# First block's output projection computed in parts during the recurrence, partial sums kept in SBUF on top of x

## The chip, the core and the metric

The kernel runs on one core of one Trainium2 chip. The metric is the device time in microseconds of the whole program. The core has five engines that work side by side and hand work over by semaphores: TensorE (PE, matmuls), VectorE (DVE), ScalarE (ACT), GpSimd (POOL) and SyncE (SP), whose queue issues most DMAs. Each engine takes its instructions in the order in which the program was laid out for it.

## The reference

Two transformer blocks over 512 tokens of 1024 channels. Only the end of the first block's mixer and the start of its feed-forward part matter here:

```python
mod = silu(c) @ ada_w + ada_b
sh1, sc1, g1, sh2, sc2, g2 = split(mod, 6)
y, _ = rwkv_scans(r, k, v, w_lo, a_lo, lp, init)        # 8 heads, forward and backward recurrence, summed
y_conv = cb * shortconv1d(cc * cx)                       # 512 channels
y_rwkv = rwkv_output(y, r, k, v, g_lo, lp)               # group norm, bonus, gate: 512 channels
out_x = concatenate([y_conv, y_rwkv], -1) @ w_out        # 1024 -> 1024
x = x + g1 * out_x
hx = modulate(rms_norm(x, norm2_g), sh2, sc2)
x = x + g2 * conv_ffn(hx)                                # up 1024 -> 2 x 2816, 3x3 conv, silu gate, down
```

## The kernel before, in words

All activations lie transposed, as eight channel tiles of 128 partitions by 512 tokens. A large product is computed from float32 operands that are each split in a rounded "hi" and a remainder "lo": `split` makes hi on ScalarE (L181) and lo on VectorE (L182), and `mm3` issues three matmuls per 128 channels, hi by hi, lo by hi and hi by lo (L169 to L171). `wsplit` loads a weight into a tile of tag "w" on SP's queue (L156) and splits it into tiles "whi" and "wlo"; there are 3 buffers of "w" and 4 of each of the others.

`rwkv` runs the recurrence in four stages of two heads each, `stage(j)` for j from 0 to 3. A stage has 12 steps g, and in each a forward (d=0) and a backward (d=1) direction. One step of one direction is a chain: matmuls into `c1` (L762 with the state, L764 with the masked matrix `AS`), a copy `R` on ScalarE (L768), L770 with `XT` into `c1`, a copy `VU` (L771), L773 into `c2`, the new state `S` on ScalarE (L775), and the output matmuls L778. Every second step `pair` prepares two chunks for a direction: loads of `BKR` on SP's queue (L732), matmuls `psc` (L735), and the masked copy into `AS` on VectorE (L737), which a later step's L764 needs. The stage's group norm `gn(j)` runs beside the next stage's steps: `ys`, `gm`, `yc`, `ysq`, `gv`, a power `grs` on GpSimd, `yc` again, a transposition `py` (L835), the gate, and a split into `ahi[4+j]`, `alo[4+j]`. That of stage 3 has nothing to run beside.

Other work is pulled from a generator `todo`, `RB[j]` pieces per step, at a priority `PF[j]` behind the step's own; a scheduler lays out each engine's instructions by these priorities. In stages 2 and 3 `todo` holds `splits` (tiles 0 to 4 of the projection's input), `ada12` (32 loads of 512 KB of the modulation weight, each followed by one product with accumulation on VectorE, L544), and `first` (weights of two outputs). These share the "w", "whi" and "wlo" buffers; `ada12`'s vector `cb` keeps one "whi" buffer as long as `ada12` is not finished. The pool with these buffers is opened when stage 1 has been issued; its space becomes free during stage 2.

Behind the stages come three pieces of `gn(3)`, then k=0..6 of the outputs n=0 and 1, then the rest of the group norm. `out_proj1` loads x into `xin` on ScalarE's queue, finishes n=0 and 1 with k=7, and does n=2 to 7 with all k in two halves of 256 columns. Per output and half: eviction with gate and residual (L924), square and sum (L887, L888). Per half: a norm factor broadcast by `rsqrt_bc`, then `nt` (L929), `ahi` (L930), `alo` (L931) for the eight tiles. `ffn_up1` begins with four units in halves (`linear_halves`), so that their first halves run while the second half of `out_proj1` is normalized, and goes on with 512-column products.

Of the kernel before, what the change touches and what calls it, by code (L numbers as in the profile page):

```python
# [10 lines left out]
F32 = mybir.dt.float32  # L11
F32R = mybir.dt.float32r
I32 = mybir.dt.int32
AF = mybir.ActivationFunctionType
ALU = mybir.AluOpType
# [3 lines left out]
P = 128  # L19
NX = 512  # L20
NC_ = 256
NT = NX + NC_
KD = 8
# [99 lines left out]
class K:  # L123
# [5 lines left out]
    MU = [i / 18 for i in range(18)]  # L129
    MH = [(2.48 + i * 0.382) / 18 for i in range(45)]  # L130
    MT = [(11.955 + i * 0.234) / 18 for i in range(32)]
    PK, PG, PF = 200, 300, (110, 105, 118, 0)
    RB, RC = (4, 2, 1, 1), 5
    psa = None

    def __init__(self, tc, A):
# [341 lines left out]
    def rwkv(self, es, ep):  # L478
        nc, r2 = self.nc, self.r2
        st = lambda name, shape: r2.tile([P] + shape, F32, name=name)  # L480
        self.BKR = [[st(f"BKR{d}{i}", [2, 2, P]) for i in range(2)] for d in range(2)]
        self.AS = [[st(f"AS{d}{i}", [2, 2, P]) for i in range(2)] for d in range(2)]
        self.R = [[st(f"R{d}{i}", [P]) for i in range(2)] for d in range(2)]
        self.S0 = [st(f"S0{d}", [P]) for d in range(2)]
        self.C1 = [self.ps2.tile([P, 2, P], F32, name=f"c1{d}") for d in range(2)]
        self.C2 = [self.ps2.tile([P, P], F32, name=f"c2{d}") for d in range(2)]
        self.VU = [[st(f"VU{d}{i}", [P]) for i in range(3)] for d in range(2)]
        for t in (self.BKR[0][0], self.BKR[1][0], self.AS[0][0], self.AS[1][0], *self.R[0], *self.R[1], *self.VU[0], *self.VU[1], *self.S0):
            nc.vector.memset(t, 0.0)
        for t in (self.BKR[0][1], self.BKR[1][1], self.AS[0][1], self.AS[1][1], self.sets[2]["XT"]):  # L490
            nc.gpsimd.memset(t, 0.0)
        todo, gn = self.todo, iter(())
        for j in range(4):
            if j < 2:
                todo = chain(todo, self.prep(j + 2))
            gn = self.stage(j, self.S[j], todo, self.RB[j], gn)
            if j == 1:
                for _ in todo:
                    pass
                ep.close()  # L500
                self.wp = self.pool(es, "wp", side="right")
                self.mmbufs, self.axbufs, self.wbufs, self.wsbufs = 6, 2, 3, 4
                pa = self.pool(self.ea, "pmix", side="right")
                self.ahi = [pa.tile([P, NX], F32R, name=f"ahi{i}") for i in range(8)]
                self.alo = [pa.tile([P, NX], F32R, name=f"alo{i}") for i in range(8)]
                todo = chain(self.splits(), self.ada12(), self.first())
                self.e3 = es.enter_context(ExitStack())
                self.psa = self.psum(self.e3, "psa", side="right")
        for _ in todo:
            pass  # L510

        for _ in range(3):
            next(gn)
        for pm, w in self.ahead:
            self.mm3(pm, [(*w(k), self.ahi[k], self.alo[k]) for k in range(7)], last=False)
        for _ in gn:
            pass

    def splits(self):
        for k in range(5):  # L520
            self.split(self.ahi[k], self.alo[k], self.zx[k])
            yield

    def first(self):
        self.ahead = []
        for n in range(2):
            self.ahead.append((self.psax(), self.wsplit(self.A["wout"][n], KD, P)))
            yield

    def ada12(self):  # L530

        nc, wp = self.nc, self.wp
        tags = [("w", self.wbufs), ("whi", self.wsbufs), ("wlo", self.wsbufs)]
        cb, sb = (wp.tile([P, 1024], F32, tag=tags[i][0], name="cb", bufs=tags[i][1]) for i in (1, 2))
        nc.sync.dma_start(out=cb, in_=self.A["cb"])
        nc.scalar.activation(out=sb, in_=cb, func=AF.Tanh, scale=0.5)
        nc.vector.tensor_scalar(out=sb, in0=sb, scalar1=0.5, scalar2=0.5, op0=ALU.mult, op1=ALU.add)
        nc.vector.tensor_tensor(out=cb, in0=sb, in1=cb, op=ALU.mult)
        acc = wp.tile([P, 32], F32, name="adacc")
        for n in range(32):  # L540
            yield
            w, t = (wp.tile([P, 1024], F32, tag=tags[i][0], name="adaw", bufs=tags[i][1]) for i in (0, 2))
            nc.sync.dma_start(out=w, in_=self.A["adat"][n])
            nc.vector.scalar_tensor_tensor(out=t, in0=w, scalar=1.0, in1=cb, op0=ALU.mult, op1=ALU.mult, accum_out=acc[:, n:n + 1])  # L544
            if n in (7, 23, 31):
                a = 0 if n == 7 else 8 if n == 23 else 24
                nc.vector.tensor_tensor(out=self.mod[:, 16 + a:17 + n, 0], in0=acc[:, a:n + 1], in1=self.v("ada_b", 16 + a, n + 1 - a), op=ALU.add)

    def prep(self, j):
        nc, pp = self.nc, self.pp  # L550
# [294 lines left out]
    def tail(self):  # L845
        nc, A = self.nc, self.A
        with ExitStack() as es:
            self.bc = self.wp.tile([P, NX], F32, name="bc")
            self.bc1 = self.wp.tile([P, NX], F32, name="bc1")
            self.rt = self.wp.tile([P, 4], F32, name="rt")  # L850
            self.xr = self.zx
            self.ps = self.psum(self.e3, "ps3", side="right")
# [38 lines left out]
    def out_proj1(self):  # L891

        nc = self.nc
        g1, sh = self.mod[:, 16:24, 0], self.mod[:, 24:32, 0]
        G = self.q.tile([P, 16], F32, name="G2")[:, 0:KD]
        nc.vector.scalar_tensor_tensor(out=G, in0=self.mod[:, 32:40, 0], scalar=1.0, in1=self.v("norm2", 0, 8), op0=ALU.add, op1=ALU.mult)
        xin = [self.q.tile([P, NX], F32, name=f"xin{k}") for k in range(KD)]
        for k in range(KD):
            nc.scalar.dma_start(out=xin[k], in_=self.A["xT"][:, k, :])
        ws = []  # L900
        for n in range(2, KD):
            if n < self.WO:
                ws.append(self.wsplit(self.A["wout"][n], KD, P))
                continue
            w = self.wp.tile([P, KD, P], F32, tag="w", name="w", bufs=self.wbufs)
            nc.sync.dma_start(out=w, in_=self.A["wout"][n])
            hi, lo = (self.q.tile([P, KD, P], F32R, name=f"wo{t}{n}") for t in "hl")
            self.split(hi, lo, w)
            ws.append(lambda k, hi=hi, lo=lo: (hi[:, k, :], lo[:, k, :]))
        H = NX // 2  # L910
        for hf in range(2):
            c = slice(H * hf, H * hf + H)
            acc = None
            for n in range(KD):
                if n < 2:
                    if hf == 0:
                        pm, w = self.ahead[n]
                        self.mm3(pm, [(*w(7), self.ahi[7], self.alo[7])], first=False)
                        nc.vector.scalar_tensor_tensor(out=self.xr[n], in0=pm, scalar=g1[:, n:n + 1], in1=xin[n], op0=ALU.mult, op1=ALU.add)
                    acc = self.sumsq(acc, self.xr[n][:, c])  # L920
                    continue
                pm = self.psmm(H)
                self.mm3(pm, [(*ws[n - 2](k), self.ahi[k][:, c], self.alo[k][:, c]) for k in range(KD)])
                nc.vector.scalar_tensor_tensor(out=self.xr[n][:, c], in0=pm, scalar=g1[:, n:n + 1], in1=xin[n][:, c], op0=ALU.mult, op1=ALU.add)  # L924
                acc = self.sumsq(acc, self.xr[n][:, c])
            bc, _ = self.rsqrt_bc(acc, H, 1.0 / 1024, 1e-6, self.q)
            for k in range(KD):
                t = self.q.tile([P, H], F32, tag="nt", name="nt", bufs=2)
                nc.vector.scalar_tensor_tensor(out=t, in0=self.xr[k][:, c], scalar=G[:, k:k + 1], in1=bc, op0=ALU.mult, op1=ALU.mult)  # L929
                nc.scalar.activation(out=self.ahi[k][:, c], in_=t, func=AF.Identity, bias=sh[:, k:k + 1])  # L930
                nc.vector.scalar_tensor_tensor(out=self.alo[k][:, c], in0=t, scalar=sh[:, k:k + 1], in1=self.ahi[k][:, c].bitcast(F32), op0=ALU.add, op1=ALU.subtract)  # L931
# [36 lines left out]
    def ffn_up1(self):  # L968
        nc, u = self.nc, self.A["fup"]
        pms = self.linear_halves([u[0], u[FF], u[1], u[FF + 1]])  # L970
        for j in range(FF):
            pg = pms.pop(0) if pms else self.linear(u[j])
            acc = self.q.tile([P, NX], F32, tag="sq", name="cv", bufs=3)
            self.conv2d(j, pg, acc)
            nc.scalar.activation(out=acc, in_=acc, func=AF.Silu)
            pv = pms.pop(0) if pms else self.linear(u[FF + j])
            nc.vector.tensor_tensor(out=acc, in0=pv, in1=acc, op=ALU.mult)
            self.split(self.hid[j][0], self.hid[j][1], acc)

# [423 lines left out]
```

## Time and profile before

| | |
|---|---|
| time, median of 3 runs | 1631.62 us (1629.88 to 1634.76) |
| time of the profiled execution | 1632.26 us |
| span of the profiled execution | 1630.5 us |
| TensorE busy | 1551.8 us, 95% |
| VectorE busy | 1011.3 us, 62% |
| ScalarE busy | 702.0 us, 43% |
| granted TensorE clock, mean | 0.981 |

The span goes from the first to the last instruction; the time has 1.8 us around it. All times within the span are counted from its start. A busy TensorE is not TensorE at its peak: the recurrence's small matmuls count as busy while they wait for each other. Two parts of the span matter here: stage 3 of the recurrence, with the work that is pulled into it, and what lies between its last matmul and the FFN's steady run.

### The profile page before, as it was taken

To read this page: it belongs to the slowest core of one execution; us is meant where nothing else is said; L and a number is where in the kernel's file an instruction comes from. 1 tells how busy PE (TensorE), PEld (TensorE's weight loads), DVE (VectorE), ACT (ScalarE), POOL (GpSimd) and SP (SyncE) were. 2 spreads that over 40 slices of the span, in tenths; PEclk is the share of its full clock that TensorE was granted. 3 is DMA by queue.
4 is the path that set the end of the run, shared out by engine and by line. 5 is a ranking of instruction groups with operands and counts; after the bars stand their busy time and mean duration, and the time that the engine had idled before them with its cause. 6 is when DMAs were issued, how large, how long until landed. Compare 5 with 4: busy or idle time off the path is not lost. (4 is left out here: it accounts for less than half of the span.)

```text
span 1630.5 us, 23350 instructions
## 1 busy us (share of the span) xinstructions
PE 1551.8 (95%) x9054; PEld 1248.5 (77%) x9054; DVE 1011.3 (62%) x1710; ACT 702.0 (43%) x1402; POOL 159.6 (10%) x221
## 2 busy tenths in 40 slices
PE   4999999999999699999999998899999999999998
PEld 2777777777777599888888887787777888888886
DVE  3435767777765677888884437678975555555221
ACT  3424445776665443333333324335554333333122
POOL 1210002131213000000000003121210000000000
PEclk9999999999999899999999999999999999999999
DMA  9243423211136742323233332221012322233321
GB/s 328 85 150 98 141 80 96 59 42 24 38 115 193 234 156 78 101 93 103 92 97 86 95 98 81 78 65 52 27 53 90 98 97 91 91 96 97 103 80 63
DMA packets 85294, 160.77 MB, mean 99 GB/s; under 512 B 24512, under 2 KB 37568, under 8 KB 85184
## 3 DMA queue, kind: packets, MB, share of 16 engines
q1 hardware_dynamic: 81152, 152.34, 29.4%
q10 hardware_dynamic: 4032, 6.94, 1.3%
q8 instruction: 71, 1.16, 0.3%
q14 instruction: 39, 0.32, 0.1%
HBM read 143.00 MB, written 7.86 MB: 93 GB/s over the span
## 5 line engine op out<-in xcount | busy, mean ns | idle before, releaser
L181 ACT ACTIVATE whi<-w 128x1024 fp32r<-128x1024 f32 (+2 forms) x220 | 208.7, 950 | 458.5 <-PE pm L170 332.7
L182 DVE TENSOR_TENSOR wlo<-w,whi 128x1024 fp32r<-128x1024 f32 (+2 forms) x212 | 229.3, 1084 | 219.9 <-ACT whi L181 213.7
L169 PE MATMUL pm<-ahi,whi 128*128 128x512 f32 (+1 forms) x624 | 237.6, 381 | 3.2 <-DVE sh L1086 2.8
L170 PE MATMUL pm<-alo,whi 128*128 128x512 f32 (+1 forms) x624 | 235.9, 378 | 0.0
L171 PE MATMUL pm<-ahi,wlo 128*128 128x512 f32 (+1 forms) x624 | 235.0, 377 | 0.0
L170 PE MATMUL pm<-al,whi 128*128 128x512 f32 x352 | 139.7, 397 | 0.0
L169 PE MATMUL pm<-ah,whi 128*128 128x512 f32 x352 | 139.2, 395 | 0.0
L171 PE MATMUL pm<-ah,wlo 128*128 128x512 f32 x352 | 139.2, 395 | 0.0
L169 PEld LDWEIGHTS pm<-ahi,whi 128*128 128x128 f32 x624 | 118.3, 190 | 24.5 <-ACT sh L1101 3.2
L171 PEld LDWEIGHTS pm<-ahi,wlo 128*128 128x128 f32 x624 | 118.3, 190 | 20.9 <-issue 0.7
L170 PEld LDWEIGHTS pm<-alo,whi 128*128 128x128 f32 x624 | 118.4, 190 | 20.5 <-issue 0.6
L959 DVE SCALAR_TENSOR_TENSOR cv<-pm,vec,cv 128x441 f32<-128x441 f32 (+2 forms) x176 | 121.1, 693 | 4.1
L170 PEld LDWEIGHTS pm<-al,whi 128*128 128x128 f32 x352 | 66.2, 188 | 16.1 <-issue 0.2
L171 PEld LDWEIGHTS pm<-ah,wlo 128*128 128x128 f32 x352 | 66.2, 188 | 16.1 <-issue 0.2
L169 PEld LDWEIGHTS pm<-ah,whi 128*128 128x128 f32 x352 | 66.2, 188 | 15.9
L171 PE MATMUL pm<-hhi,wlo 128*128 128x512 f32 x176 | 72.5, 412 | 2.7 <-DVE wlo L182 2.7
L169 PE MATMUL pm<-hhi,whi 128*128 128x512 f32 x176 | 72.6, 413 | 0.2 <-ACT whi L181 0.2
L170 PE MATMUL pm<-hlo,whi 128*128 128x512 f32 x176 | 71.6, 407 | 0.0
L171 PE MATMUL pd<-whi,gl 128*128 128x512 f32 x176 | 69.3, 394 | 0.0
L169 PE MATMUL pm<-hh,whi 128*128 128x512 f32 x176 | 69.3, 394 | 0.0
L170 PE MATMUL pm<-hl,whi 128*128 128x512 f32 x176 | 69.3, 394 | 0.0
L171 PE MATMUL pm<-hh,wlo 128*128 128x512 f32 x176 | 69.3, 394 | 0.0
(403 smaller groups left out, 3082.8 us busy)
## 6 DMA issues: line engine op xcount, KB each, us to landing
w<-in_fup SPq DMA_DIRECT2D x44, 512.0 KB, 3.4
adaw<-in_adat SPq DMA_DIRECT2D x32, 512.0 KB, 4.4
w<-in_win SPq DMA_DIRECT2D x44, 256.0 KB, 2.8
w<-in_wg SPq DMA_DIRECT2D x22, 512.0 KB, 3.4
w<-in_wu SPq DMA_DIRECT2D x22, 512.0 KB, 3.4
w<-in_wd SPq DMA_DIRECT2D x22, 512.0 KB, 3.7
w<-in_win SPq DMA_DIRECT2D x18, 512.0 KB, 3.3
w<-in_wout SPq DMA_DIRECT2D x16, 512.0 KB, 3.5
```

The source lines that it names most:

```text
L169: nc.tensor.matmul(out, lh, rh, start=(first and i == 0), stop=False)
L170: nc.tensor.matmul(out, lh, rl, start=False, stop=False)
L171: nc.tensor.matmul(out, ll, rh, start=False, stop=(last and i == n - 1))
L181: self.nc.scalar.activation(out=hi, in_=src, func=AF.Copy)
L182: (eng or self.nc.vector).tensor_tensor(out=lo, in0=src, in1=hi.bitcast(F32), op=ALU.subtract)
L959: nc.vector.scalar_tensor_tensor(out=o, in0=p[:, ro[0] + dr:ro[1] + dr, co[0] + dc:co[1] + dc], scalar=w(i), in1=o, op0=ALU.mult, op1=ALU.add)
```

## The change

`fill` takes the place of `splits`, `ada12` and `first` as the filler of stages 2 and 3. It splits the tiles 0 to 4 and loads x again into the tiles that become free (`base`; three more tiles are new), with an `ada12` step each. Then it computes the output projection of all eight n in two passes, k=0..3 and k=4,5: a part of the weight is loaded and split, 12 or 6 matmuls of 512 columns go into a PSUM tile, and VectorE adds the tile, scaled by the gate g1, onto `base[n]`, followed by one `ada12` step. Last it loads and splits k=6 and 7 of all n in two tiles (`wlast`). `RB` and `PF` give two pieces a step in stages 2 and 3, and in stage 3 the same priority offset as in stage 2. `out_proj1` is left with k=6,7: six matmuls for each output and half, added to `base`. Its weight loads and the reload of x on ScalarE's queue go away. The last eight `ada12` steps move into `ffn_up1`.

```diff
-    PK, PG, PF = 200, 300, (110, 105, 118, 0)
-    RB, RC = (4, 2, 1, 1), 5
+    PK, PG, PF = 200, 300, (110, 105, 118, 118)
+    RB, RC = (4, 2, 2, 2), 5
...
-                todo = chain(self.splits(), self.ada12(), self.first())
+                self.mods = self.ada12()
+                todo = self.fill()
...
-        for _ in range(3):
-            next(gn)
-        for pm, w in self.ahead:
-            self.mm3(pm, [(*w(k), self.ahi[k], self.alo[k]) for k in range(7)], last=False)
...
+    def fill(self):
+        part = lambda n, k0, k1: self.wsplit(self.A["wout"][n][:, k0:k1], k1 - k0, P)
+        self.base = self.zx[0:5] + [self.wp.tile([P, NX], F32, tag=t, name="base", bufs=1) for t in ("bc", "bc1", "base")]
         for k in range(5):
             self.split(self.ahi[k], self.alo[k], self.zx[k])
+            nc.sync.dma_start(out=self.base[k], in_=self.A["xT"][:, k, :])
+            next(self.mods)
+            yield
+        for k in range(5, 8):
+            nc.sync.dma_start(out=self.base[k], in_=self.A["xT"][:, k, :])
+            next(self.mods)
+            yield
+        for k0, k1 in ((0, 4), (4, 6)):
+            for n in range(KD):
+                w = part(n, k0, k1)
+                pm = self.psax()
+                self.mm3(pm, [(*w(k - k0), self.ahi[k], self.alo[k]) for k in range(k0, k1)])
+                yield
+                nc.vector.scalar_tensor_tensor(out=self.base[n], in0=pm, scalar=self.mod[:, 16 + n:17 + n, 0], in1=self.base[n], op0=ALU.mult, op1=ALU.add)
+                next(self.mods)
+                yield
+        self.wlast = []
+        for i in range(2):
+            w = self.wp.tile([P, KD, P], F32, tag="w", name="w", bufs=self.wbufs)
+            nc.sync.dma_start(out=w.rearrange("p (n k) c -> p n k c", k=2), in_=self.A["wout"][4 * i:4 * i + 4, :, 6:8, :].rearrange("n p k c -> p n k c"))
...
-        for k in range(KD):
-            nc.scalar.dma_start(out=xin[k], in_=self.A["xT"][:, k, :])
...
                 pm = self.psmm(H)
-                self.mm3(pm, [(*ws[n - 2](k), self.ahi[k][:, c], self.alo[k][:, c]) for k in range(KD)])
-                nc.vector.scalar_tensor_tensor(out=self.xr[n][:, c], in0=pm, scalar=g1[:, n:n + 1], in1=xin[n][:, c], op0=ALU.mult, op1=ALU.add)
+                self.mm3(pm, [(*self.wlast[n](k), self.ahi[k][:, c], self.alo[k][:, c]) for k in (6, 7)])
+                nc.vector.scalar_tensor_tensor(out=self.xr[n][:, c], in0=pm, scalar=g1[:, n:n + 1], in1=self.base[n][:, c], op0=ALU.mult, op1=ALU.add)
...
             pv = pms.pop(0) if pms else self.linear(u[FF + j])
+            if j > 2:
+                next(self.mods, None)
```

The lines of the recurrence move down by 18 with the change: L770 becomes L788, L764 L782, L737 L755. On TensorE, in steps 2 and 3 of stage 3 before (c10 and c11 are the two directions' `c1`), the rows of the recurrence stand one behind the other:

```order
L770 MATMUL c10_2328<-R00_2322,XT0_83 64x64 x2
L764 MATMUL c11_2329<-VU12_2337,AS11_2321 64x64 x2
L766 MATMUL c21_2331<-S01_2327,cst_60 128x128
L773 MATMUL c20_2330<-VU02_2334,kbt_4807 128x128
L770 MATMUL c11_2329<-R10_2324,XT0_83 64x64 x2
L762 MATMUL c10_2328<-S00_2326,KR00_86 64x128
L773 MATMUL c21_2331<-VU12_2337,kbt_4818 128x128
L764 MATMUL c10_2328<-VU00_2332,AS01_2319 64x64 x2
```

At the same place of the changed kernel, on TensorE, px_4780 and px_4856 are the sums of the sixth and the seventh part:

```order
L171 MATMUL px_4780<-ahi3_4156,wlo_4777 128x512
L791 MATMUL c20_2330<-VU02_2334,kbt_5046 128x128
L782 MATMUL c11_2329<-VU12_2337,AS11_2321 64x64 x2
L169 MATMUL px_4856<-ahi0_4153,whi_4852 128x512
L170 MATMUL px_4856<-alo0_4161,whi_4852 128x512
L780 MATMUL c10_2328<-S00_2326,KR00_86 64x128
L788 MATMUL c11_2329<-R10_2324,XT0_83 64x64 x2
L782 MATMUL c10_2328<-VU00_2332,AS01_2319 64x64 x2
L171 MATMUL px_4856<-ahi0_4153,wlo_4853 128x512
```

Step 2's backward L788 now stands behind two matmuls of the seventh part. Its forward L788 stands in the fifth and the sixth part, step 3's forward one behind the ninth part, and step 6's behind five of the six matmuls of the fifteenth.

On VectorE, in stage 3 before, the masked copies for steps 6 and 7 (L737 into AS01 and AS11) stand between products of `ada12` (L544):

```order
L836 SCALAR_TENSOR_TENSOR zx_65<-py_4975,vec_61,zx_65 128x512
L544 SCALAR_TENSOR_TENSOR adaw_5077,adacc_4440<-adaw_5076,cb_4434 128x1024
L737 COPY_PREDICATED AS01_2319<-cst_60,psc_4985 128x512
L544 SCALAR_TENSOR_TENSOR adaw_5133,adacc_4440<-adaw_5132,cb_4434 128x1024
L737 COPY_PREDICATED AS11_2321<-cst_60,psc_4996 128x512
```

On VectorE of the changed kernel, at the same copies (L755), L182 is the split of a weight part, L535 the addition of a part's sum onto `base` or its reused tile, and L561 the product of `ada12`:

```order
L182 TENSOR_TENSOR wlo_5340<-w_5337,whi_5339 128x256
L535 SCALAR_TENSOR_TENSOR base_4227<-px_5268,mod_62,base_4227 128x512
L561 SCALAR_TENSOR_TENSOR adaw_5352,adacc_4239<-adaw_5351,cb_4233 128x1024
L182 TENSOR_TENSOR wlo_5388<-w_5385,whi_5387 128x256
L755 COPY_PREDICATED AS01_2319<-cst_60,psc_5280 128x512
L854 SCALAR_TENSOR_TENSOR zx_65<-py_5256,vec_61,zx_65 128x512
L561 SCALAR_TENSOR_TENSOR adaw_5400,adacc_4239<-adaw_5399,cb_4233 128x1024
L755 COPY_PREDICATED AS11_2321<-cst_60,psc_5291 128x512
```

The copy for step 6 stands behind the split of the sixteenth and last part (wlo_5388). The split of the first part stands behind stage 2's group norm up to its second `yc`.

## Rows read from the trace of the kernel before

**Rows 1.** Page, part 1: busy time, share of the span, instructions.

```profile
PE 1551.8 (95%) x9054; PEld 1248.5 (77%) x9054; DVE 1011.3 (62%) x1710; ACT 702.0 (43%) x1402; POOL 159.6 (10%) x221
```

**Rows 2.** Windows view, all engines; clock, DMA share, GB/s last.

```profile
core 0: us, PE busy (x) PEld busy (x) DVE busy (x) ACT busy (x) POOL busy (x), PEclk, DMA share, GB/s
491.00:551.60 60.60, 59.11 (x456) 44.13 (x454) 35.77 (x62) 35.64 (x121) 16.25 (x22) 1.00 0.64 199
551.60:564.00 12.40, 0.07 (x1) 0.10 (x2) 9.87 (x21) 1.96 (x3) 1.64 (x1) 0.66 0.76 236
564.00:569.60 5.60, 5.60 (x17) 4.43 (x18) 3.99 (x6) 1.69 (x2) 0.00 (x0) 0.54 0.88 278
626.40:640.00 13.60, 13.60 (x112) 13.43 (x111) 8.48 (x13) 5.54 (x6) 0.00 (x0) 1.00 0.27 86
640.00:860.00 220.00, 220.00 (x972) 182.09 (x971) 188.66 (x252) 81.32 (x104) 0.00 (x0) 1.00 0.30 97
```

**Rows 3.** Timeline of TensorE; start, duration, what ran, idle before it.

```profile
492.18 0.45 PE L770 MATMUL c<-R,XT 128*64 128x64 f32 x4
...
504.48 0.45 PE L770 MATMUL c<-R,XT 128*64 128x64 f32 x4
...
521.66 0.45 PE L770 MATMUL c<-R,XT 128*64 128x64 f32 x4
...
551.12 0.45 PE L778 MATMUL c<-VU,AS 128*64 128x64 f32 x4 [0.36 <-ACT VU L771]
...
563.93 0.66 PE L835 MATMUL py<-cst,yc 128*128 128x128 f32 x2 [12.36 <-DVE yc L831]
```

**Rows 4.** Windows view, VectorE's instructions of line L544 alone.

```profile
491.00:551.60 60.60, 25.33 (x41) 1.00 0.64 199
551.60:564.00 12.40, 6.42 (x12) 0.66 0.76 236
```

**Rows 5.** Waits of SP's queue, 460 to 630: total, times, longest.

```profile
SPq L543 <- DVE adaw L544: 40.1, 19, 4.7
```

**Rows 6.** Timeline of VectorE.

```profile
494.63 0.69 DVE L818 TENSOR_REDUCE gm<-ys 128x8 f32<-128x512 f32 x1 [1.52 <-POOL ys L815]
...
505.43 0.69 DVE L831 TENSOR_TENSOR yc<-yc,grs 128x512 f32<-128x512 f32 x1 [2.50 <-POOL grs L830]
...
569.09 0.69 DVE L182 TENSOR_TENSOR alo<-zx,ahi 128x512 fp32r<-128x512 f32 x1 [0.62 <-ACT ahi L181]
...
595.22 0.48 DVE L924 SCALAR_TENSOR_TENSOR zx<-pm,mod,xin 128x256 f32<-128x256 f32 x1 [1.43 <-PE pm L171]
...
599.55 0.87 DVE L929 SCALAR_TENSOR_TENSOR nt<-zx,G,nbc 128x256 f32<-128x256 f32 x2 [0.79 <-PE nbc L208]
```

**Rows 7.** Page, part 6: DMA issues, KB each, median us to landing.

```profile
adaw<-in_adat SPq DMA_DIRECT2D x32, 512.0 KB, 4.4
...
w<-in_win SPq DMA_DIRECT2D x44, 256.0 KB, 2.8
```

**Rows 8.** VectorE by line and form, 467 to 660: busy, mean ns.

```profile
L544 DVE SCALAR_TENSOR_TENSOR adaw<-adaw,cb 128x1024 f32<-128x1024 f32 x32 | 39.7, 1253 | 4.0 <-DMA adaw<-in_adat 4.0
...
L182 DVE TENSOR_TENSOR wlo<-w,whi 128x1024 fp32r<-128x1024 f32 x15 | 18.3, 1223 | 11.2 <-ACT whi L181 10.9
...
L931 DVE SCALAR_TENSOR_TENSOR alo<-nt,mod,ahi 128x256 fp32r<-128x256 f32 x16 | 7.1, 482 | 0.9 <-ACT ahi L930 0.9
...
L929 DVE SCALAR_TENSOR_TENSOR nt<-zx,G,nbc 128x256 f32<-128x256 f32 x16 | 7.0, 476 | 1.6 <-PE nbc L208 1.6
...
L888 DVE TENSOR_TENSOR acc<-acc,sq 128x256 f32<-128x256 f32 x14 | 5.8, 421 | 2.7 <-ACT sq L887 2.7
...
L924 DVE SCALAR_TENSOR_TENSOR zx<-pm,mod,xin 128x256 f32<-128x256 f32 x12 | 5.8, 481 | 4.0 <-PE pm L171 3.8
```

**Rows 9.** DMA issues of 467 to 563, KB each, median us to landing.

```profile
BKR<-KR SPq DMA_DIRECT2D x16, 64.0 KB, 3.3
...
BKR<-KR SPq DMA_DIRECT2D x4, 32.0 KB, 5.6
```

More of the change, by code (lines that the diff above doesn't have):

```diff
@@ L510, in rwkv @@
             pass
-        for _ in range(3):
-            next(gn)
-        for pm, w in self.ahead:
-            self.mm3(pm, [(*w(k), self.ahi[k], self.alo[k]) for k in range(7)], last=False)
         for _ in gn:
             pass
-    def splits(self):
+    def fill(self):
+        nc = self.nc
+        part = lambda n, k0, k1: self.wsplit(self.A["wout"][n][:, k0:k1], k1 - k0, P)
+        self.base = self.zx[0:5] + [self.wp.tile([P, NX], F32, tag=t, name="base", bufs=1) for t in ("bc", "bc1", "base")]
         for k in range(5):
             self.split(self.ahi[k], self.alo[k], self.zx[k])
+            nc.sync.dma_start(out=self.base[k], in_=self.A["xT"][:, k, :])
+            next(self.mods)
             yield
[L524 to L527, printed above, removed]
+        for k in range(5, 8):
[15 more added lines that the diff above has]
+            nc.sync.dma_start(out=w.rearrange("p (n k) c -> p n k c", k=2), in_=self.A["wout"][4 * i:4 * i + 4, :, 6:8, :].rearrange("n p k c -> p n k c"))
+            hi, lo = (self.wp.tile([P, KD, P], F32R, tag=f"w{t}", name=f"w{t}", bufs=self.wsbufs) for t in ("hi", "lo"))
+            self.split(hi, lo, w)
+            self.wlast += [lambda k, hi=hi, lo=lo, n=n: (hi[:, 2 * n + k - 6, :], lo[:, 2 * n + k - 6, :]) for n in range(4)]
             yield
@@ L540, in ada12 @@
         for n in range(32):
-            yield
             w, t = (wp.tile([P, 1024], F32, tag=tags[i][0], name="adaw", bufs=tags[i][1]) for i in (0, 2))
@@ L847, in tail @@
         with ExitStack() as es:
-            self.bc = self.wp.tile([P, NX], F32, name="bc")
-            self.bc1 = self.wp.tile([P, NX], F32, name="bc1")
+            self.bc = self.wp.tile([P, NX], F32, tag="bc", name="bc", bufs=1)
+            self.bc1 = self.wp.tile([P, NX], F32, tag="bc1", name="bc1", bufs=1)
             self.rt = self.wp.tile([P, 4], F32, name="rt")
@@ L896, in out_proj1 @@
         nc.vector.scalar_tensor_tensor(out=G, in0=self.mod[:, 32:40, 0], scalar=1.0, in1=self.v("norm2", 0, 8), op0=ALU.add, op1=ALU.mult)
-        xin = [self.q.tile([P, NX], F32, name=f"xin{k}") for k in range(KD)]
-        for k in range(KD):
-            nc.scalar.dma_start(out=xin[k], in_=self.A["xT"][:, k, :])
[L900 to L909, printed above, removed]
         H = NX // 2
@@ L914, in out_proj1 @@
             for n in range(KD):
[L915 to L921, printed above, removed]
                 pm = self.psmm(H)
-                self.mm3(pm, [(*ws[n - 2](k), self.ahi[k][:, c], self.alo[k][:, c]) for k in range(KD)])
-                nc.vector.scalar_tensor_tensor(out=self.xr[n][:, c], in0=pm, scalar=g1[:, n:n + 1], in1=xin[n][:, c], op0=ALU.mult, op1=ALU.add)
+                self.mm3(pm, [(*self.wlast[n](k), self.ahi[k][:, c], self.alo[k][:, c]) for k in (6, 7)])
+                nc.vector.scalar_tensor_tensor(out=self.xr[n][:, c], in0=pm, scalar=g1[:, n:n + 1], in1=self.base[n][:, c], op0=ALU.mult, op1=ALU.add)
                 acc = self.sumsq(acc, self.xr[n][:, c])
```

## The prediction

> **What bounds the kernel now.** The page gives TensorE 95% of the span [rows 1], so I looked for the stretch where it is not doing useful work and cut the program there with the windows view [rows 2]. From 640 to 860 us (the FFN's up projection) TensorE is full: 972 matmuls in 220.00 us, 0.226 us for a 512-column matmul at full clock, with VectorE at 188.66. Between the last recurrence matmul (551.12, ended at 551.6) and the first matmul behind it (563.93, after 12.36 us idle) [rows 3] nothing can run, as only the group norm of stage 3 is left; VectorE is busy 9.87 of those 12.40 us [rows 2], and 6.42 of that are `ada12` products (L544) [rows 4]. Then comes `out_proj1` up to 640.
>
> In stage 3 itself, 491 to 551.6, TensorE's busy figure is 59.11 of 60.60 [rows 2], but it holds only 456 instructions: the recurrence is a chain TensorE, ScalarE, TensorE. Step 0 has its L770 at 492.18, step 3 at 504.48, step 6 at 521.66, the end is at 551.6 [rows 3]: 4.1 us a step at first, and 29.9 from step 6 to the end. The filler is not free either: SP stood 40.1 us in 19 waits for a tile that VectorE had not yet read (L543 behind L544) [rows 5], with three "w" buffers.
>
> **The change, part by part.** Its sign is a difference of two numbers: how much later the recurrence ends, and how much less is left behind it.
>
> *What it puts into stage 3.* Sixteen parts: 8 outputs with k=0..3 (12 matmuls each) and 8 with k=4,5 (6 each), 144 × 0.226 = 32.6 us of TensorE. Each brings a load, a split on ScalarE and VectorE, an addition on VectorE and an `ada12` step. Although `fill` is available from stage 2 on, the pool opens late there, so nearly all of it falls into stage 3. TensorE's order shows the serious part: step 2's L788 stands inside the 5th to 7th part, step 3's behind the 9th, step 6's first behind the 15th. VectorE's shows pair 3's masked copy, which step 6 needs, behind the 16th split. An engine that takes its rows in order then ties the recurrence to the fill.
>
> When does the 16th split come? *Start.* The first split stands behind stage 2's group norm, whose `gm` starts at 494.63 and whose last `yc` ends at 506.1 now [rows 6]. Two products and a copy fewer lie in that chain then (3 us), one product and the split behind it (2 us): about 504. *Pace.* Three buffers carry two loads per part. A product's buffer is held for 4.4 us of landing [rows 7] and 1.25 of VectorE [rows 8], 5.65; a 256 KB part for 2.8 [rows 7] and two conversions of about 0.69 (the 569.09 row [rows 6]; ScalarE's taken like it), 4.2. With about 1 us of hand-overs that is 10.85 over 3 buffers, 3.6 us per part. Before, these buffers allowed a product each (4.4 + 1.25) / 3 = 1.9 us, and 41 records, two to a product, in 60.6 us [rows 4] make 2.95, as SP also waits for the recurrence's own loads; so I take 4.0 for the first eight. The halves of the second pass land in 2.8 (256 KB [rows 7]) to 3.3 us (64 KB [rows 9]) and split in 0.42 (as L888's 128x256 row [rows 8]): 5.65 + 3.05 + 0.84 + 1 over 3, 3.5, taken as 3.6. The 16th split then is at 504 + 8 × 4.0 + 7 × 3.6 = 561. Bounds: below, VectorE's own work, 1.25 + 0.69 + 0.69 and 1.25 + 0.42 + 0.69 per part, together 40 us, so 544; above, every landing as slow as the 5.6 us of the 32 KB loads in this stretch [rows 9], (5.6 + 1.25 + 5.6 + 1.4 + 1) / 3 = 4.95 × 15, so 578.
>
> From there: masked copy and step 6's first matmuls to its L788 1.6, then five steps and 2.4 for the rest of the last. A step is 4.1 where little lies beside it and (29.9 - 2.4) / 5 = 5.5 from step 6 on now [rows 3]; I take the middle, 4.8, as products and the last parts still lie there: 26.4. The recurrence ends at 589 instead of 551.6, **37.4 us later** (4.1: 33.9, 5.5: 40.9).
>
> Here a rule stands against the change. Step 3's L770 rows ran at 504.48 as soon as their data came [rows 3], with no held matmul ahead of them. The Trainium skill ("TensorE: Matmul & The Clock Gate", section "Architectural detail: the array is 16× 32×32, not 1× 128×128") says that TensorE's queue can pull weight loads ahead of matmuls in flight but is otherwise no free reordering, and that VectorE is strictly first in, first out. By it the recurrence waits for the parts as above, and the sum stands. Without holding, the parts would cost the recurrence at most ScalarE's sixteen splits ahead of its copies, 8 × 0.69 + 8 × 0.42 = 9 us: 9 - 29.4 = -20.4, about 1611.
>
> *What it takes from behind.* (1) Group norm: no products in its chain, 12.36 less 6.42 [rows 3, 4], **6.4 us**. (2) From the last `alo` (569.09 + 0.69 = 569.8 [rows 6]) to 640 are 70.2 us. Now 6 instead of 24 matmuls remain per output and half, and VectorE sets the pace: 16 evictions of 0.481, 14 sums of 0.421, 16 each of `nt` and `alo` at 0.48 (0.476 and 0.482) make 28.9 [rows 8], two weight splits of the FFN at 1.223 make 2.4, start 1.0. The chain between the halves shows 595.22 + 0.48 to 599.55 [rows 6], 3.85, in which two sums (0.84) and two small rows (about 0.5) ran: 2.5 idle, twice. Sum 37.3 to the last normalized tile. Behind it now lie 13.6 us [rows 2]; then the second halves of three units, 3 × 24 matmuls of 256 columns at 0.12, are 8.6, and 1.3 for a weight buffer that `cb` still holds. So 47.2 instead of 70.2, **23.0 us**; at 13.6 behind it, 19.3. (3) The reload of x moves from ScalarE's queue to SP's, where the loads of `fill` wait anyway: in the pace.
>
> *What it moves further.* Eight products go to `ffn_up1`: 8 × 1.25 = 10 us on VectorE, which has 220.00 - 188.66 = 31 us free there [rows 2]. I take nothing; if no gap could be used it would be 10.
>
> **Sum.** +37.4 - 6.4 - 23.0 = +8.0. The profiled execution took 1632.26, so 1640.3; on the median of three, 1631.62, it is 1639.6. A difference of 0.3% (4.9 us) is about what a measurement of this kernel can tell from none. Break-even is a recurrence that ends 29.4 us late, that is a 16th split at 553.
>
> **Rivals.**
> - *The fill runs at VectorE's pace.* If landings overlap better than three buffers suggest, the 16th split comes at 544, the recurrence ends at 572, 20.4 late: 9 us gained, about 1623. For it: the DMA share of 0.64 in stage 3 leaves room [rows 2]. Against: SP's 40.1 us of waits for buffers [rows 5]. If ready recurrence matmuls were also not held, the time would be the 1611 worked out above. The rival holds from a 16th split before 548: 0.24.
> - *Balance.* Split between 548 and 558, end of the sum within 4.9 us of zero, 1627 to 1636: 0.20.
> - *Much slower.* TensorE falls to half clock. Where it waited for VectorE (551.6 to 564) the granted clock was 0.66, and 0.54 after it to 569.6 [rows 2], the lower level of 1.2 GHz; a 512-column matmul then takes about 0.45. In stage 3 twelve of them would take 5.4 us, more than the 4.0 of pace: eight times 1.4 is 11 us, 1650. In the tail, where TensorE now waits for VectorE, the 72 last matmuls would cost 8.6 more, 1648. Slow landings (578) give 1656. Against the clock falling: in stage 3 it was 1.00 throughout [rows 2]. The Trainium skill, same page, section "HAM oscillation — how this bites in real kernels", describes bursts of matmuls between waits for loads that pay for the cold array each time; 12 matmuls (2.7 us) and a pause of 1.3 look like it, but the recurrence lies between them. 0.14.
>
> **How the numbers follow.** The forecast (16th split between 558 and 570) has 0.42, and its own range is 1636.5 to 1648. Faster 0.24, same 0.20, slower 0.42 + 0.14 = 0.56. The range of 8 in 10 goes from 1619 (a little beyond VectorE's pace) to 1652.
>
> **What would show it.** Step 3's L788 near 537 to 542 instead of 504.5; SP's waits for "w" buffers as the largest; pair 3's copy directly behind the 16th split at about 561; last L796 at about 589; then 6 us less to the first `py`, and about 47 us from the last `alo` to where the FFN's 512-column matmuls run without gaps; in the FFN no new wait of TensorE for VectorE. I am wrong if parts follow each other at 3 us or less, if recurrence matmuls run far ahead of the parts that stand before them, or if the tail takes more than 52 us.

## The result and the profile after

The changed kernel takes 1641.79 us (median of 4 runs, 1641.57 to 1643.09) against 1631.14 us: a ratio of 1.0062, 95% interval 1.0047 to 1.0077. It is slower by 10.7 us; 8.0 were forecast. The span of the profiled execution is 1639.9 us, 9.4 more than before.

The timeline of TensorE shows the recurrence of stage 3 and what follows it; the rows answer to [rows 3], and L788, L796, L853 are the old L770, L778, L835.

```profile
493.56 0.45 PE L788 MATMUL c<-R,XT 128*64 128x64 f32 x4
497.62 0.45 PE L788 MATMUL c<-R,XT 128*64 128x64 f32 x4
...
519.57 0.33 PE L788 MATMUL c<-R,XT 128*64 128x64 f32 x2
...
522.92 0.33 PE L788 MATMUL c<-R,XT 128*64 128x64 f32 x2
...
534.76 0.45 PE L788 MATMUL c<-R,XT 128*64 128x64 f32 x4
...
560.08 0.45 PE L788 MATMUL c<-R,XT 128*64 128x64 f32 x4
...
590.73 0.45 PE L796 MATMUL c<-VU,AS 128*64 128x64 f32 x4 [0.36 <-ACT VU L789]
598.03 1.08 PE L853 MATMUL py<-cst,yc 128*128 128x128 f32 x4 [6.86 <-DVE yc L849]
...
647.99 0.40 PE L169 MATMUL pm<-ahi,whi 128*128 128x512 f32 x1
```

These are steps 0, 1, 2 (in two halves), 3 and 6, the end of the recurrence, the first matmul behind it, and the first 512-column matmul of the FFN, which stood at 639.00 before. The recurrence ends at 591.2 instead of 551.6. TensorE then idles 6.86 us instead of 12.36.

The timeline of VectorE has the first, ninth and sixteenth split of a weight part, the masked copy that step 6 needs, and the last tile of the input and of the output of `out_proj1`:

```profile
504.62 0.69 DVE L182 TENSOR_TENSOR wlo<-w,whi 128x512 fp32r<-128x512 f32 x1
...
532.16 0.42 DVE L182 TENSOR_TENSOR wlo<-w,whi 128x256 fp32r<-128x256 f32 x1
...
556.71 0.42 DVE L182 TENSOR_TENSOR wlo<-w,whi 128x256 fp32r<-128x256 f32 x1
557.04 0.73 DVE L755 COPY_PREDICATED AS<-cst,psc 128x512 f32<-128x512 int32 x1
...
601.33 0.69 DVE L182 TENSOR_TENSOR alo<-zx,ahi 128x512 fp32r<-128x512 f32 x1 [0.70 <-ACT ahi L181]
...
637.48 0.94 DVE L929 SCALAR_TENSOR_TENSOR alo<-nt,mod,ahi 128x256 fp32r<-128x256 f32 x2 [0.19 <-ACT ahi L928]
```

The windows view, with the columns of [rows 2], shows stage 3, the group norm's stretch, `out_proj1` and the FFN:

```profile
500.00:520.00 20.00, 16.47 (x79) 12.48 (x80) 13.63 (x26) 4.95 (x11) 1.94 (x2) 1.00 0.69 215
520.00:540.00 20.00, 20.00 (x105) 15.42 (x106) 14.31 (x25) 6.78 (x19) 1.81 (x3) 1.00 0.74 229
540.00:560.00 20.00, 19.96 (x137) 15.57 (x135) 14.38 (x26) 9.62 (x31) 1.99 (x5) 1.00 0.59 186
560.00:580.00 20.00, 19.73 (x158) 14.77 (x156) 9.24 (x12) 13.80 (x41) 3.10 (x7) 1.00 0.48 156
591.20:598.20 7.00, 0.17 (x1) 0.20 (x2) 3.79 (x7) 0.90 (x2) 1.64 (x1) 0.59 0.00 0
...
602.00:638.40 36.40, 32.80 (x218) 31.07 (x218) 28.02 (x70) 15.70 (x34) 1.39 (x2) 0.85 0.09 30
660.00:860.00 200.00, 200.00 (x884) 165.58 (x883) 177.42 (x243) 74.09 (x94) 0.00 (x0) 1.00 0.38 121
```

In stage 3 TensorE is busy throughout from 520 on, with fewer instructions per 20 us while the parts run. Before, it also filled `out_proj1`, as the windows view of that kernel shows from the input's last tile on:

```profile
569.80:626.40 56.60, 55.66 (x423) 53.41 (x422) 37.90 (x75) 23.34 (x42) 1.39 (x2) 1.00 0.38 126
```

Now it no longer does (32.80 of 36.40). VectorE is busy almost throughout from 605 to 625, and the clock falls again behind that:

```profile
605.00:625.00 20.00, 16.39 (x113) 14.83 (x113) 18.28 (x47) 11.18 (x24) 0.69 (x1) 0.93 0.01 1
625.00:630.00 5.00, 5.00 (x25) 5.00 (x25) 1.69 (x4) 0.00 (x0) 0.69 (x1) 0.50 0.66 210
```

The FFN stays full although VectorE has more to do there.

By stretches, in us: the recurrence ends 39.6 later; from there to the last `alo` of the input (602.0) it is 10.8 instead of 18.2; from there to the FFN's first 512-column matmul 46.0 instead of 69.2; from that to the end of the span 991.9 instead of 991.5. Sum: +39.6 - 7.4 - 23.2 + 0.4 = +9.4.

### The profile page after: what moved, and what is told of

The parts are those of the page before. It is cut to its first block, busy times and chain, and to the rows that moved or that the text cites. A ratio compares the mean times of both kernels' runs of the same rounds, so it can differ in the third digit from the quotient of the medians.

```text
span 1639.9 us, 23242 instructions
## 1 busy us (share of the span) xinstructions
PE 1557.0 (95%) x8958; PEld 1247.7 (76%) x8958; DVE 1021.9 (62%) x1738; ACT 704.3 (43%) x1412; POOL 155.0 (9%) x221
## 5 line engine op out<-in xcount | busy, mean ns | idle before, releaser
L181 ACT ACTIVATE whi<-w 128x1024 fp32r<-128x1024 f32 (+3 forms) x234 | 215.1, 920 | 471.5 <-PE pm L170 337.2
L182 DVE TENSOR_TENSOR wlo<-w,whi 128x1024 fp32r<-128x1024 f32 (+3 forms) x226 | 235.8, 1045 | 219.2 <-ACT whi L181 213.7
L169 PE MATMUL pd<-whi,gh 128*128 128x512 f32 x176 | 69.5, 395 | 0.0
```

Of the source, the lines that this page charges most:

```text
L169: nc.tensor.matmul(out, lh, rh, start=(first and i == 0), stop=False)
L181: self.nc.scalar.activation(out=hi, in_=src, func=AF.Copy)
L182: (eng or self.nc.vector).tensor_tensor(out=lo, in0=src, in1=hi.bitcast(F32), op=ALU.subtract)
```

## The experiments

"Stage 3" is here the time from step 0's first L770 (L788) to the end of the last output matmul, read from the timeline of TensorE; it does not contain shifts from earlier stages. It is 59.4 us before and 97.6 after, each from one profiled execution. In the run with twelve float32 matmuls behind it, where the stage itself is as before, it is 59.4 again; in the run with six of them in the changed kernel it is 99.2, with a granted clock of 0.82 up to 510 instead of 1.00. Differences of that size in the changed kernel say nothing.

**Late fill.** The parts stand evenly between the steps.

```diff
-    PK, PG, PF = 200, 300, (110, 105, 118, 118)
+    PK, PG, PF = 200, 300, (110, 105, 2400, 400)
```

> The changed kernel with one edit: pieces of the fill that are pulled in stage 2 get their place 2400 (twelve steps) later instead of 118, those of stage 3 400 later. In TensorE's order the parts then stand evenly between the steps of stage 3: step 3 behind none or one of them instead of nine, step 11 behind fifteen. Theory O (order): the recurrence was late because its rows stood behind parts, which follow each other at the 3.4 us that three buffers give; then step 3's L788 comes before 512, the recurrence ends within 10 us of the last split, at 560 to 572 instead of 591, and the time is 1611 to 1623. Rival W (work): TensorE, VectorE and ScalarE have no room for the fill beside the recurrence in whatever order; then the end stays at 585 to 595 and the time at 1636 to 1645.

Measured: 1635.73 us, ratio to before 1.0032 (1.0020 to 1.0045), so it recovers half of the loss. But the rows say that neither theory had the place:

```profile
484.57 0.45 PE L788 MATMUL c<-R,XT 128*64 128x64 f32 x4 [0.19 <-ACT R L786]
...
578.82 0.45 PE L796 MATMUL c<-VU,AS 128*64 128x64 f32 x4
592.66 1.09 PE L853 MATMUL py<-cst,yc 128*128 128x128 f32 x4 [8.96 <-DVE yc L849]
```

Stage 3 still takes 94.7 us, with 134 of the 144 matmuls in it. What is gained is its start, 484.57 instead of 493.56: stage 2, from its first L788 to that of stage 3, took 62.6 us instead of 68.7, and the other 2.9 us were there when stage 2 began, where the edit changes nothing. Order within stage 3 was worth at most 3 us, not the 19 to 31 of theory O, and 2.3 of these are the ten matmuls that fell behind the stage's end.

**Three matmuls per part**, to take TensorE's share out.

```diff
-                self.mm3(pm, [(*w(k - k0), self.ahi[k], self.alo[k]) for k in range(k0, k1)])
+                self.mm3(pm, [(*w(k - k0), self.ahi[k], self.alo[k]) for k in (k0,)])
```

> The changed kernel with 3 matmuls in each part instead of 12 or 6 (the sums lack the other channels); loads, splits, additions and products stay. Theory O with the pace set by the three buffers: the splits still follow each other at 3.2 to 3.5 us, the 16th comes at 552 to 558, the recurrence ends at 583 to 592, the time is 1632 to 1643. Rival T (TensorE's own matmuls, 2.7 us of each 3.4 us, hold the recurrence): up to 96 x 0.226 = 22 us less, the recurrence ends at 569 to 575, the time is 1617 to 1624.

Measured: 1627.73 us in one run, between the two ranges. The recurrence ends at 574.6, where T had it, but the splits follow each other at 4.3 us and the sixteenth comes at 566.84, not at O's 552 to 558. Stage 3 is 82.9 us, 14.7 less than after, for 96 matmuls or 21.7 us less. It is still 23.5 above before with only 10.9 us of parts on TensorE. The windows view shows where the rest lies:

```profile
491.70:510.00 18.30, 13.35 (x77) 8.91 (x74) 11.93 (x22) 7.33 (x23) 5.23 (x7) 0.81 0.51 171
510.00:530.00 20.00, 19.82 (x127) 14.57 (x127) 12.86 (x20) 11.07 (x34) 2.86 (x6) 0.92 0.62 195
530.00:550.00 20.00, 19.99 (x135) 14.16 (x135) 14.73 (x25) 11.15 (x36) 2.25 (x6) 1.00 0.62 188
```

TensorE idles 5 us up to 510 and 6.9 in the whole stage (1.5 in the 60.6 us of [rows 2]), and its clock, 1.00 in the profile of the changed kernel, is 0.81 up to 510 and 0.92 up to 530. An estimate from these rows is 10.9 of parts, 5.4 of idle and up to 5.1 of clock (0.19 of 18.3 us and 0.08 of 20), some 21 of the 23.5 us. From 530 to 566 TensorE is full again. So this run doesn't show that the pace of the splits holds the recurrence, and its clock makes it a rough measure of TensorE's share.

**No products with the parts**, to take the buffers' share out.

```diff
                 nc.vector.scalar_tensor_tensor(out=self.base[n], in0=pm, scalar=self.mod[:, 16 + n:17 + n, 0], in1=self.base[n], op0=ALU.mult, op1=ALU.add)
-                next(self.mods)
                 yield
...
-        for n in range(32):
+        for n in (*range(8), *range(24, 32)):
```

> The changed kernel without the sixteen ada12 steps that go with the parts (no load, no product; the second half's modulation values are taken as the bias alone). Theory O with the pace set by three buffers: each part then needs one buffer instead of two, so the pace is left to TensorE, 2.7 and 1.5 us, and the 16th split comes at about 537 to 542 instead of 557; the recurrence ends at 570 to 577, the time is 1619 to 1627. Rival T (TensorE's matmuls alone set the pace): the 16th split stays at 552 or later and the time at 1634 to 1643.

Measured: 1637.99 us in one run, the time of T and not of O, though the sixteenth split came between the two. VectorE's timeline shows the splits of the first pass, TensorE's the next step of the recurrence and its end:

```profile
508.20 1.28 DVE L182 TENSOR_TENSOR wlo<-w,whi 128x512 fp32r<-128x512 f32 x2
...
510.92 0.68 DVE L182 TENSOR_TENSOR wlo<-w,whi 128x512 fp32r<-128x512 f32 x1
...
519.08 0.68 DVE L182 TENSOR_TENSOR wlo<-w,whi 128x512 fp32r<-128x512 f32 x1
```

```profile
532.12 0.40 PE L788 MATMUL c<-R,XT 128*64 128x64 f32 x4
...
588.09 0.45 PE L796 MATMUL c<-VU,AS 128*64 128x64 f32 x4 [0.36 <-ACT VU L789]
```

With the buffers relieved the parts follow each other at 2.72 us, the length of twelve matmuls (12 × 0.226), the first pass is done by 530, and the sixteenth split comes at 545.96 instead of 556.71. The recurrence simply stood still until 532 and ended at 588.5 all the same. Stage 3 is 96.8 us, though in this run the clock was 0.91 up to 510. The pace of the parts was not what the lag came from.

**Products in the FFN, alone**, in the kernel before.

```diff
-from itertools import chain
+from itertools import chain, islice
...
-                todo = chain(self.splits(), self.ada12(), self.first())
+                self.mods = self.ada12()
+                todo = chain(self.splits(), islice(self.mods, 25), self.first())
...
             pv = pms.pop(0) if pms else self.linear(u[FF + j])
+            if j > 2:
+                next(self.mods, None)
```

> The kernel before with one part of the change alone: the last eight ada12 products go to the FFN's up projection. By the sum of the prediction the group norm's stretch loses 6.4 us and the FFN gives nothing back: 1624 to 1626. Rival: the FFN has no gaps for them on VectorE and takes up to 10 us back, 1631 to 1635. Second rival: the weight buffers come free earlier as well and out_proj1 also gains, below 1623.

Measured: 1620.94 us, ratio 0.9942 (0.9930 to 0.9954): the second rival. The weights of outputs 0 and 1 are there eight products earlier, and their 42 matmuls, which stood behind the first `py` in TensorE's order, now stand ahead of it and fill the group norm's idle stretch. The windows view of that stretch, and TensorE's timeline at its end:

```profile
554.50:563.60 9.10, 9.10 (x41) 6.96 (x41) 4.92 (x8) 2.36 (x5) 1.64 (x1) 1.00 0.64 200
```

```profile
563.25 0.39 PE L171 MATMUL px<-ahi,wlo 128*128 128x512 f32 x1
563.67 0.63 PE L836 MATMUL py<-cst,yc 128*128 128x128 f32 x4
```

From the end of the recurrence to the FFN's first 512-column matmul it is 74.6 us instead of 87.4. In this profile the recurrence ended 4.1 us later than in that of before, and the FFN's part of the span is unchanged (991.2 us against 991.5), which leaves 9.0 us of the span. If the two parts of the change simply added up, the move of the projection alone would cost about 20 us (10.7 + 9.5); no run has it alone, and in the changed kernel there are no such matmuls to fill the stretch.

**Bare matmuls.** In the kernel before, and in that kernel without its products, matmuls on resident tiles were added to stage 3, with no load, split or addition.

```diff
+            if j == 3:
+                with self.prio(at + 118):
+                    self.mm3(self.psax(), [(self.ahi[k][:, 0:P], self.alo[k][:, 0:P], self.ahi[k], self.alo[k]) for k in range(4)])
```

With 144:

> The kernel before with 144 matmuls of 512 columns more in stage 3, twelve behind each step, on tiles that are resident, into PSUM tiles that nothing reads: the parts' TensorE work without their loads, splits, additions. Theory W (TensorE is full in stage 3 already, the parts' 32.6 us add to it): the recurrence ends 30 to 36 us later, at 582 to 588. Theory C (the recurrence is a chain with gaps, as the prediction read it, and what held it was the pace of the weights): the matmuls find room, the recurrence ends at 552 to 565. The time follows less up to 10 us, since the weights of the first two outputs are then there early, as in the run with the products in the tail.

With 48 (the same lines under `if j == 3 and g % 3 == 2`):

> The same with 48 such matmuls, twelve behind each third step, 10.9 us of TensorE. W: the recurrence ends 9 to 13 us later, at 560 to 565. C: 551 to 555.

With the products left out and no added matmul:

```diff
-                todo = chain(self.splits(), self.ada12(), self.first())
+                nc.vector.tensor_copy(out=self.mod[:, 16:48, 0], in_=self.v("ada_b", 16, 32))
+                todo = chain(self.splits(), self.first())
```

> The kernel before with all 32 ada12 loads and products left out (the modulation values are taken as the bias alone), so that next to nothing runs beside the recurrence of stage 3. Theory W (the recurrence fills TensorE by itself): from step 0 to the end it takes 56 to 60 us, against 59.4 with the products. Theory C (a chain that the products and loads on VectorE and SP hold up): clearly less, below 54 us.

And with both edits:

> The same with 144 matmuls of 512 columns spread over stage 3, and no loads or products at all. W: those that run within the stage add their length less some 3 us, as in the run with the products beside them; with 110 to 130 of them the stage takes 78 to 88 us. C: below 68 us.

Not all the added matmuls ran within stage 3; those that did are counted in the table, from TensorE's timeline (extra time is against 59.4 us; for the last row against 59.9).

| kernel | 512-column matmuls in stage 3 | their length, × 0.226 us | stage 3 | extra |
|---|---|---|---|---|
| before | 0 | 0 | 59.4 | |
| products left out | 7 | 1.6 | 59.9 | 0.5 |
| 48 bare | 28 | 6.3 | 62.5 | 3.1 |
| 144 bare | 113 | 25.5 | 81.8 | 22.4 |
| 144 bare, products left out | 112 | 25.3 | 81.7 | 21.8 |
| after | 144 | 32.6 | 97.6 | 38.2 |
| no products with the parts | 144 | 32.6 | 96.8 | 37.4 |

The absolute ends of the two bare runs (570.7 and 545.2) lay below what W gave, because a part of the matmuls ran outside stage 3 and stage 3 began earlier (488.9 and 482.7; in the second run 6.1 us of this were there when stage 2 began). The lengths agree with W: bare matmuls cost their own length less 2 to 3 us, whether products lie beside them or not (in the last row 105 matmuls, or 23.7 us, more than with the products left out cost 21.8). The run with nothing beside the recurrence shows why, in the windows view:

```profile
485.00:545.00 60.00, 59.80 (x465) 45.59 (x463) 11.73 (x19) 37.01 (x126) 10.98 (x24) 1.00 0.09 28
```

VectorE is down to 11.73 of 60 us and the DMA share to 0.09, and the stage takes as long as ever, with TensorE at 59.80. Times of the four in single runs: 1642.20, 1626.36, 1610.27 and 1637.24 us.

A busy share alone doesn't settle this, and blocks of twelve matmuls in an engine that takes its rows in order would also delay a chain with gaps. So it matters whether TensorE waits between the recurrence's rows. Its timeline in the run with nothing beside the recurrence:

```profile
504.25 0.45 PE L771 MATMUL c<-R,XT 128*64 128x64 f32 x4
504.62 0.49 PE L763 MATMUL c<-S,KR 128*128 128x128 f32 x2
505.04 0.45 PE L765 MATMUL c<-VU,AS 128*64 128x64 f32 x4
505.42 0.49 PE L774 MATMUL c<-VU,kbt 128*128 128x128 f32 x2
```

And in the run with 144 bare matmuls and no products, right behind a block of them:

```profile
524.98 0.38 PE L763 MATMUL c<-S,KR 128*128 128x128 f32 x2
525.20 0.39 PE L767 MATMUL c<-S,cst 128*128 128x128 f32 x2
```

The single records, which the timeline merges, can be counted. In the first run the distance from one record's start to the next hardly depends on anything but their shapes: 0.152 us from the last record with a 64-wide weight tile (128*64) to one with a 128-wide tile, 0.205 the other way. Over the stage's 454 records only 1.2 us lie above the usual distance (the median) of such a pair, and in the kernel before 3.7. So TensorE waits for next to nothing there: the recurrence fills it by itself, and its small matmuls don't count as busy because they wait for each other. But the columns alone don't fill it. Rows with the same weight width follow each other faster, as the second fence shows: from L763 to the next row it is 0.22 us there, and 0.42 between L771 and L765. At the distances that records of one width have among themselves (0.058 us for 64 columns, 0.11 for 128, 0.217 for 256) the stage would take some 42 us, an estimate; most of the other 18 go with its 107 changes between 64- and 128-wide weight tiles. Whether an order with fewer changes is quicker, no run shows.

**Where TensorE is free.** Twelve float32 matmuls that read stage 3's output tile, in the kernel before:

```diff
+        if j == 3:
+            for i in range(12):
+                nc.tensor.matmul(self.psax(), self.c("ident"), Y[1].rearrange("p n v -> p (n v)"), start=True, stop=True)
```

> The kernel before with twelve float32 matmuls of 512 columns (some 6 to 11 us of TensorE) that read stage 3's output tile and so can only run in the group norm's idle stretch; nothing reads their result. Both theories: they are free there, the first py at 563 to 565 as now, and the clock behind it stays at 1.00, so the time is 0 to 3 us below the kernel before. If they cost their length, TensorE was not what this stretch had to spare: 1636 to 1641.

Measured: ratio 0.9988 (0.9973 to 1.0002). TensorE's timeline:

```profile
554.47 0.45 PE L778 MATMUL c<-VU,AS 128*64 128x64 f32 x4 [0.36 <-ACT VU L771]
555.27 10.57 PE L818 MATMUL px<-Y,cst 128*128 128x512 f32 x24 [0.36 <-ACT Y L188]
567.22 0.44 PE L838 MATMUL py<-cst,yc 128*128 128x128 f32 x2 [1.38 <-DVE yc L834]
```

10.57 us of matmuls cost nothing in this stretch; bare matmuls within stage 3 cost nearly their length. (This profile's stage 3 began 3.3 us later than that of before, so its first `py` is read from the end of the recurrence: 12.3 us, as before.) The granted clock behind the stretch was 1.00 (567.2 to 572.3) instead of 0.54, and still the time is the same within the interval.

**TensorE kept busy in the changed kernel's idle stretch**, with six of these matmuls:

```diff
+        if j == 3:
+            for i in range(6):
+                nc.tensor.matmul(self.psax(), self.c("ident"), Y[1].rearrange("p n v -> p (n v)"), start=True, stop=True)
```

> The changed kernel with six such float32 matmuls (3 to 6 us) in its own idle stretch of 6.9 us, so that TensorE does not come out of it at half clock. If the low clock (0.85 over 602 to 638) is part of the loss: 2 to 5 us less than the changed kernel, 1637 to 1640. If VectorE sets the pace there, as the prediction had it: within 1.5 us of 1641.8.

Measured: 1637.67 us, ratio to before 1.0041 (1.0026 to 1.0055); against the changed kernel's 1.0062 the intervals overlap. In the profile the granted clock of the following stretch is 0.95 over 600.7 to 634.8 instead of 0.85, and from the last `alo` of the input to the FFN's first 512-column matmul it is 43.7 us instead of 46.0. So the low clock at the start of this stretch is about 2.3 us of the loss in these two profiles, and the rest of the 4 us between the medians is not settled. A second fall remains in both kernels (0.50 over 625 to 630 in the changed one, 0.66 over 620 to 625 here); what it costs no run shows.

**Better versions.** The late fill had shown stage 2 shorter by 6.1 us. Both runs build on the products in the FFN.

```diff
-    RB, RC = (4, 2, 1, 1), 5
+    RB, RC = (4, 2, 0, 3), 5
```

> The kernel before with the last eight products in the FFN, and no filler pulled in stage 2 but three pieces a step in stage 3. If the filler that starts in stage 2's ninth step costs that stage some 5 to 7 us (12.2 us between its steps 8 and 9 before, 7.1 in the run with the late fill), stage 3 starts at 484 to 488 and the time is 1613 to 1618. If the filler only takes the same time elsewhere: 1619 to 1624.

```diff
-    PK, PG, PF = 200, 300, (110, 105, 118, 0)
+    PK, PG, PF = 200, 300, (110, 105, 1200, 0)
```

> The same, with the filler pulled in stage 2 left at one piece a step, but its place 1200 (six steps) later. As above: 1613 to 1618 if stage 2 is spared, 1619 to 1624 if the filler only takes its time elsewhere.

Measured: 1619.47 us, ratio 0.9922 (0.9908 to 0.9935), and 1615.07 us, ratio 0.9894 (0.9878 to 0.9910). With three pieces a step stage 3 starts at 484.6, as expected, and stage 2 is down to 62.8 us from 69.7, but stage 3 takes 69.7. With the pieces six steps later stage 2 is 64.5 and stage 3 59.2: the best version measured, faster than both kernels.

What costs stage 2 its time shows in ScalarE's rows between its steps 8 and 9, here before:

```profile
467.91 3.23 ACT L181 ACTIVATE ahi<-zx 128x512 fp32r<-128x512 f32 x6
471.11 1.06 ACT L536 ACTIVATE cb<-cb 128x1024 f32<-128x1024 f32 x1
472.20 0.63 ACT L775 ACTIVATE S<-c,pc 64x64 f32<-64x64 f32 x2
```

Six `ahi` splits and the row of `cb` run in one block, and the recurrence's new state `S` stands behind them. From step 8's first L770 to step 9's it takes 12.1 us. With all products left out it is 11.4, behind the same six splits and a weight's split; in the best version 9.0, behind four splits (2.19 us); in the late fill and with three pieces a step 7.1, behind one (0.63 us). So it goes with the splits that stand together on ScalarE ahead of the recurrence, and not with the products.

## Why the prediction was right in its number, and which step failed

- **Start and pace of the parts:** the first split was forecast at 504 and came at 504.6, the ninth at 536 (532.2), the sixteenth at 561 (556.7). The parts followed at 3.4 to 3.5 us, near the 3.6 and 3.5 of the buffers without my allowance for collisions. The run without the products, 2.72 us in the first pass, speaks for the buffers; the one with three matmuls per part, 4.3 with the same loads, says that they weren't all.
- **Step 3 behind the ninth part:** forecast 537 to 542, measured 534.8. Step 2's L788, in two halves at 519.57 and 522.92, ran between matmuls of parts, as the order had them. The Trainium skill ("TensorE: Matmul & The Clock Gate", section "Architectural detail: the array is 16× 32×32, not 1× 128×128") calls TensorE's queue a partial reorder window, which can pull weight loads ahead of matmuls in flight. The trace agrees in so far as these matmuls kept the order of the program.
- **End of the recurrence:** forecast 589, measured 591.2, but not by the way forecast. From the sixteenth split it took 34.5 us instead of 28: 3.4 instead of 1.6 to step 6's L788, and 31.1 instead of 26.4 from there, 5.75 a step and not 4.8. The 5.5 that I had read from step 6 on was the recurrence's own rate and not the filler's doing: with the products left out it takes 34.4 us from step 6 to the end, and 11.3 for the first three steps. Those are shorter by construction, as the first four steps work on chunks of half the width and have no output matmuls.
- **The step that failed** is the reading of stage 3: "it holds only 456 instructions: the recurrence is a chain". From this I took TensorE to have room, and made the lag a matter of three buffers and of order. The 59.11 of 60.60 us meant that it had none, as the distances between its rows show. With TensorE full, 32.6 us of parts must add nearly 32.6 us, in whatever order and with however many buffers: order was worth at most 3 us, the products with their buffers 0.8 (both close to what the stage varies by), bare matmuls cost their length less 2 to 3. Real parts cost 5.6 us more than their length; 3.5 us of idle show in 500 to 520, most of it while TensorE waits for a part's weights. That the number came out is luck. The sixteenth split came 4.3 us earlier than forecast and the way from there took 6.5 us longer, and the end doesn't hang on that split: without the products it came 10.8 us earlier still, and the recurrence ended only 2.6 us earlier.
- **Group norm:** forecast 6.4 us, measured 7.4. **Tail:** the last normalized tile came 36.4 us behind the last input tile (37.3 forecast), the FFN's start after 46.0 instead of 69.2, 23.2 us gained (23.0 forecast). From 605 to 625 VectorE sets this pace (18.28 of 20 us); around that TensorE runs at half clock (0.50 at 602 to 605 and at 625 to 630), which the sum didn't have, so the close fit of the tail is in part luck. Of the rival with the clock, 0.85 came true in the tail, of which the first fall cost some 2.3 us; in stage 3 the clock stayed at 1.00 in this profile, but was 0.82 up to 510 in the run with six matmuls, whose stage took 1.6 us longer.
- **FFN:** nothing forecast, 0.4 us measured, and nothing in the run with this part alone.
- **Why it is slower at all:** before, both stage 3 and `out_proj1` are bound by TensorE. Moving 32.6 us of matmuls from one to the other gains nothing in itself. It lengthened stage 3 by 38 us, and behind it only 23 came back, because there VectorE took over as the bound and the clock fell. The one stretch in which TensorE had time, the group norm's, was left idle for 6.86 us.
- **What I had missed of the rest:** the move of the products is worth 9.5 us in the kernel before, not 6.4, since it lets matmuls into that idle stretch.

## What to carry to other kernels

A stage of small matmuls with a busy share near 100% can be full even if its instructions are few and form a chain; two directions that run side by side fill each other's gaps. Before work is moved under such a stage, run it once with bare matmuls of the same length added, and once with everything else taken out, and look whether the engine's rows follow each other at distances that depend on their shapes alone. Move work to the stretch where the engine idles (here 12 us behind the recurrence), and count what bounds the place from which the work is taken: there the gain ends when the next engine takes over.

## What the runs showed of the hardware

- The small float32 matmuls of the recurrence (128x64, four records in 0.45 us) keep TensorE busy: with VectorE at 11.73 and TensorE at 59.80 of 60 us, 105 bare matmuls more, of 23.7 us, made the stage 21.8 us longer.
- A change between a 64-wide and a 128-wide weight tile takes TensorE's time: the next start came 0.152 us (to 128) or 0.205 us (to 64) behind the last, against 0.058 and 0.11 between records of 64 and 128 columns without a change.
- A float32 matmul of 512 columns shows as two records and took 0.88 us (24 records in 10.57 us for twelve), against 0.226 for one of the split operands.
- After 7 us with TensorE nearly idle (granted clock 0.59) it ran at 0.50, the lower level of 1.2 GHz, for 3.8 us; with 5.42 us of matmuls in that stretch the clock was 1.00 throughout.
